# Ordering the engines' instructions by the library's detailed machine model

## The chip, the cores and the metric

The kernel runs on one core of a Trainium2 chip. The metric is the device time of one execution in microseconds (us), a median over runs.

## What is computed

Three blocks of a diffusion-style network run one after the other on 512 latent tokens and 256 context tokens of width 1024: a retention and state-space mixer with a gated feed-forward, an attention block with a feed-forward, and a second model's block with a recurrence over time, a short convolution and sixteen experts that each choose 64 tokens. Cut to the order of the work:

```python
h_lat = h_lat + m_lat[2] * retention_ssd_mixer(...)        # block 0, also for the context
h_lat = h_lat + m_lat[5] * swiglu(modulate(rms_norm(h_lat), ...), w_gate, w_up, w_down)
h_lat = h_lat + m_lat[2] * mla_mixer(...)                  # block 1
h_lat = h_lat + m_lat[5] * swiglu(...)
x = rms_norm(h_lat, final_norm_w)
x = x + g1 * (concat([rwkv_out(...), short_conv(...)]) @ w_out)   # second block
x = x + g2 * expert_choice_ffn(modulate(rmsnorm(x), ...), router_w, w_gate, w_up, w_down)
return rmsnorm(x)
```

## The kernel before

The kernel is traced once, as straight-line code, and nothing in it is a loop on the chip. Activations lie transposed, 128 features on the partitions and tokens along the free axis. Most products are made in three passes from a high and a low part of both operands: `gemm` issues the passes (L430, L432, L435), and `split_to` makes the parts, the high one on ScalarE (`act`, L382) and the low one on VectorE (`tt`, L385; on GpSimd where the caller says so). All helpers record their instructions under their own line, so L382, L385 and L388 (`stt`) stand for many places.

Memory is handed out by the kernel's own code while it is traced. `_Arena` gives out stretches of SBUF and `_Banks` gives out the eight banks of PSUM, both in the order of the trace. A stretch that was freed and given out again makes its next writer wait for its last reader. All loads and stores are issued by SyncE (`load`, L400; the experts' weights, L2594), so they form one queue in order.

Work that may overlap is traced interleaved: `braid` and `weave` step several generators at fixed rates, and `step` puts pieces of side work (`ada_rows`, which reads the transposed modulation weights `wadt` and sums products on VectorE, L668) between the blocks of the feed-forward `ffn`. `ffn` works in groups of hidden blocks (`FFG`, six groups for each of two layers). Each group ends with the loads of its down weights (`wdown`).

Further lines that are named below:
- `ssd` in block 0: L1282 multiplies the masked scores of a chunk with the values, behind a decay chain over VectorE, ScalarE and GpSimd (`affine_select`, L1266 and L1268); L1301 is the state's product there. L952 to L954 are the value projection's products that run beside it.
- `rwkv_prep` in the second block: L1957 multiplies a masked product with the values; the mask is applied by GpSimd (L385 on POOL). L1897 and L1909 are its copies and chunk products.
- `tri_inverse`: VectorE inverts triangular blocks with transposes (L2014, L2029, L2037, L2038), and L2045 and L2055 combine the blocks on TensorE.
- `moe`: the experts' products (L2598) with weights that stream in.

The order in which each engine gets its instructions is not the traced order. When the trace is closed, the library plays the traced instructions on a model of the machine: an engine of the model takes, among the instructions whose operands are ready there, the one that was traced first. The order that comes out of this play is written into each engine's program and is fixed from then on. On the chip every engine goes through its program in order and waits on semaphores. Without a further argument the library uses its simple model.

Of the kernel before, what the change touches and what calls it, by code (L numbers as in the profile page):

```python
# [167 lines left out]
def _run(g):  # L168
    """a generator to its end -> what it returns"""
    try:  # L170
        while True:
            next(g)
    except StopIteration as e:
        return e.value


def _parts(t):
    """two ranges of tokens"""
    return [(0, TL), (TL, TA)] if t == TA else [(0, TC), (TC, TL)]


class _Hook:
    """a generator step by step; what it returns"""
# [19 lines left out]
class _Arena:  # L203
    """SBUF, float32 left of a movable bound and float32r right of it, each side a stack of tiles.
    Long-lived buffers lie at the outer ends, transient ones rotate near the bound.
    Zones set memory aside for work that other work is to overlap."""
# [37 lines left out]
    def move(self, mid, *cuts):  # L244
        """float32 up to mid floats, float32r behind; new tiles end at the cuts"""
# [18 lines left out]
    def reserve(self, z, n, dt=F32, below=SIZE):  # L264
        """set n floats aside for zone z"""
# [48 lines left out]
    def forget(self, n):  # L314
        """the order of the last releases alone counts from here on"""
# [45 lines left out]
class _K:  # L361
# [50 lines left out]
    def prefetch(self, key, src):  # L412
        """split weights ahead of their use"""
        self.pre[key] = self.wsplit(src, top=True)
# [10 lines left out]
    def gemm(self, w, nk, acts, outs):  # L425
        """outs: list of (psum AP, token slice); w: function (hi|lo, k) -> lhsT; acts: list of (hi, lo) per k"""
# [22 lines left out]
    def rstd_cols(self, cols, n, scale, eps, op=OP.add):  # L449
        """1 / sqrt(cols * scale <op> eps), with a Newton step behind the square root's table"""  # L450
# [11 lines left out]
    def rms_bcast(self, acc, t, nfeat):  # L462
        """acc [128, t]: sums of squares per partition; -> bank with 1/rms on every partition"""
# [9 lines left out]
    def col_bcast(self, r, n):  # L473
        """[128, n] -> bank with the n * 128 values along each partition"""
# [6 lines left out]
    def sumsq(self, blocks, t, w=None, bufs=None, pool=None):  # L481
        """sum over blocks of squares, [128, t]; with w a second one, of the blocks times columns of w"""
# [21 lines left out]
    def modulate(self, xs, t, pb, segs, us=None, dve=()):  # L504
        """xs: list of f32 [128, t]; segs: list of (slice, scale fn(k), shift fn(k)); us: two APs for the normed values or
        None; -> list of (hi, lo) Bufs"""
# [17 lines left out]
    def norm_parts(self, xs, t, nfeat, segs, pool=0, low=((), ())):  # L524
        """normed and modulated blocks, range of tokens by range -> list of (hi, lo) Bufs"""
# [12 lines left out]
    def modulate_part(self, outs, xs, t0, t1, r, segs, low=()):  # L538
        """low: the blocks whose low part is left to GpSimd"""
# [22 lines left out]
    # log1p(e) for 0 <= e <= 1, elementwise on small tiles  # L562
# [31 lines left out]
    def ada(self, parts, w=2):  # L594
        """parameters of layer 0 -> Buf [128, 48, 2]: block-major vectors, (latent, context); params 1 and 4 are 1 + scale"""
# [30 lines left out]
    def ada_first(self, h):  # L626
        """half h of the blocks of layer 0's first shift and scale"""
# [15 lines left out]
        # block 8 j + 4 h + n at column (n, j, v)  # L643
# [8 lines left out]
    def ada_rows(self):  # L652
        """the same for layers 1 and 2 (context: shift and scale 0 alone), as VectorE's sums of products along the rows of
        the transposed weights"""
# [37 lines left out]
    # ---------------------------------------------------------------- layer 0  # L692
# [49 lines left out]
    def gated(self, x, p, P, gate, n, t0, t1, two):  # L742
        """x += gate * p over a range of tokens"""
# [5 lines left out]
    def out_proj(self, w, y, T, x, P, gate, k0=0, name=None, hook=None):  # L749
        """x += gate * (rows k0... of w)^T y; with a hook range of tokens by range, and the hook behind each"""  # L750
# [28 lines left out]
    def step(self, g, n, z=1):  # L779
        """n steps of work in a zone"""  # L780
# [8 lines left out]
    def ffn(self, l, P, T, x, a, side, rate, start=0, hook=None):  # L789
        """x += gate * swiglu(a); a: normed blocks as (hi, lo) Bufs; the last sums range of tokens by range, with a hook  # L790
        behind each"""
# [5 lines left out]
        def outs(bg, bu, bc, t0, t1):  # L797
            """gate's and up's PSUM over a range of tokens"""
# [27 lines left out]
        for g, nb in enumerate(FFG):  # L826
            j0 = 0
            last = g == len(FFG) - 1
            if g == 0:
                # the first two blocks range by range: the second range's norm is under way  # L830
# [55 lines left out]
    def mixer0(self, ab, P):  # L886
# [7 lines left out]
        # dt, [16, tokens]  # L894
# [1846 lines left out]
```

## Time and profile before

| | |
|---|---|
| median of 3 runs | 3152.22 us (3151.61 to 3154.9) |
| span of the profiled execution | 3154.1 us |
| TensorE busy | 2976.9 us (94%) |
| VectorE busy | 1702.1 us (54%) |
| ScalarE busy | 989.3 us (31%) |
| GpSimd busy | 312.5 us (10%) |
| mean granted TensorE clock | 0.947 |
| read from HBM | 441.35 MB |

The profile is of one execution. [...] A wait row names the waiting engine and line, and behind the arrow what came last of the things it waited for. A timeline row stands for one or more instructions of one line and one form in a row; the bracket gives the idle time of the engine ahead of it. "SPq" is the issue of a DMA by SyncE.

### The profile page before, as it was taken

The numbers are of one execution on the slowest core, as the hardware profiler recorded it, in microseconds if no ns is written. First come the engines' busy times: TensorE is split into PE (matmuls) and PEld (weight loads), VectorE is DVE, ScalarE is ACT, GpSimd is POOL, SyncE is SP. The second block draws the span as 40 slices with busy tenths as digits, with TensorE's granted clock in tenths as the row PEclk, the third lists the DMA queues.
The fourth block names the chain that finished last, engine by engine and source line by source line (L and its number), as shares of the span: only waits on it lengthen the run. The fifth ranks groups of instructions, "written<-read, shape, count | busy, mean of one in ns | idle before, by whom it ended". The sixth has DMA issues, their size and how long they took to land.

```text
span 3154.1 us, 43364 instructions
## 1 busy us (share of the span) xinstructions
PE 2976.9 (94%) x17688; PEld 2113.3 (67%) x17688; DVE 1702.1 (54%) x2713; ACT 989.3 (31%) x1625; POOL 312.5 (10%) x287
## 2 busy tenths in 40 slices
PE   7999999999999989999999999988899998999997
PEld 4776558888888877554788777775675565344443
DVE  5865557675764355565755762388636734112113
ACT  5421445412121165333544422244323313000001
POOL 0124310000000010111000000002201311000000
PEclk9999999999999999999999999888888877999999
DMA  6334451474563031001322222131113124999998
GB/s 216 106 103 124 137 175 58 152 257 157 165 226 134 11 125 40 22 22 45 108 95 74 95 79 75 34 108 64 55 38 106 41 85 173 377 409 409 409 409 303
DMA packets 170584, 458.97 MB, mean 146 GB/s; under 512 B 20320, under 2 KB 52704, under 8 KB 170000
## 3 DMA queue, kind: packets, MB, share of 16 engines
q1 hardware_dynamic: 170384, 456.19, 41.0%
q8 instruction: 139, 2.28, 0.3%
q14 instruction: 61, 0.50, 0.0%
HBM read 441.35 MB, written 14.78 MB: 145 GB/s over the span
## 4 chain that ended last, share of the span: by engine, by line
PE 71%; DVE 9%; DMA 5%; issue 3%; ACT 3%; POOL 2%; SPq 0%; DVEq 0%; POOLq 0%; ACTq 0%
PE ps L430 13%; PE ps L432 12%; PE ps L435 12%; PE ps L2598 9%; DVE mem L385 4%; ACT mem L382 3%; PE ps L1614 3%; PE ps L1773 2%; PE ps L2581 2%; DMA mem<-in_wadt_dram 2%; DVE mem L388 1%; POOL mem L385 1%; PE ps L1771 1%; PE ps L606 1%; PE ps L2258 1%
## 5 line engine op out<-in xcount | busy, mean ns | idle before, releaser
L382 ACT ACTIVATE mem<-mem 128x1024 fp32r<-128x1024 f32 (+16 forms) x802 | 543.2, 707 | 850.0 <-PE ps L435 225.3
L385 DVE TENSOR_TENSOR mem<-mem,mem 128x1024 fp32r<-128x1024 f32 (+13 forms) x595 | 515.5, 882 | 394.3 <-ACT mem L382 197.4
L382 ACT ACTIVATE mem<-ps 128x512 f32<-128x512 f32 (+8 forms) x627 | 321.0, 525 | 1130.8 <-PE ps L435 318.4
L430 PE MATMUL ps<-mem,mem 128*128 128x512 f32 (+3 forms) x1991 | 601.4, 359 | 16.1 <-ACT mem L382 13.1
L432 PE MATMUL ps<-mem,mem 128*128 128x512 f32 (+2 forms) x1906 | 569.4, 354 | 1.0 <-DVE mem L385 0.9
L435 PE MATMUL ps<-mem,mem 128*128 128x512 f32 (+2 forms) x1977 | 417.8, 352 | 0.0
L430 PEld LDWEIGHTS ps<-mem,mem 128*128 128x128 f32 (+2 forms) x1991 | 339.9, 189 | 88.0 <-ACT mem L382 19.6
L432 PEld LDWEIGHTS ps<-mem,mem 128*128 128x128 f32 (+1 forms) x1906 | 327.9, 189 | 59.9 <-issue 5.9
L435 PEld LDWEIGHTS ps<-mem,mem 128*128 128x128 f32 (+1 forms) x1977 | 323.7, 189 | 56.2 <-issue 4.1
L2598 PE MATMUL ps<-mem,mem 128*64 128x512 f32 x1344 | 309.2, 598 | 1.0 <-ACT mem L382 0.5
L385 POOL TENSOR_TENSOR mem<-mem 128x256 f32<-128x256 f32 (+4 forms) x84 | 106.1, 1269 | 1810.6 <-ACT mem L382 1411.2
L432 PE MATMUL ps<-mem 128*128 128x512 f32 (+1 forms) x814 | 275.1, 368 | 1.4 <-POOL mem L385 1.0
L430 PE MATMUL ps<-mem 128*128 128x512 f32 (+1 forms) x729 | 258.2, 378 | 10.1 <-ACT mem L382 7.8
L385 DVE TENSOR_TENSOR mem<-mem,ps 128x512 f32<-128x512 f32 (+5 forms) x234 | 128.9, 582 | 236.0 <-PE ps L2598 103.5
L385 DVE TENSOR_TENSOR mem<-mem 128x256 f32<-128x256 f32 (+19 forms) x347 | 186.6, 546 | 85.3 <-ACT mem L382 36.2
L2598 PEld LDWEIGHTS ps<-mem,mem 128*64 128x64 f32 x1344 | 107.1, 137 | 177.9 <-issue 165.7
L385 POOL TENSOR_TENSOR mem<-mem,mem 128x512 f32<-128x512 f32 (+6 forms) x108 | 145.3, 1357 | 515.4 <-ACT mem L382 402.1
L432 PEld LDWEIGHTS ps<-mem 128*128 128x128 f32 x814 | 154.9, 197 | 30.9 <-issue 4.4
L435 PE MATMUL ps<-mem 128*128 128x512 f32 (+3 forms) x743 | 170.7, 359 | 0.0
L430 PEld LDWEIGHTS ps<-mem 128*128 128x128 f32 x729 | 141.5, 199 | 43.5 <-ACT mem L382 12.7
L385 DVE TENSOR_TENSOR mem<-ps,mem 128x512 f32<-128x512 f32 (+6 forms) x176 | 114.2, 664 | 98.3 <-PE ps L1107 37.0
L388 DVE SCALAR_TENSOR_TENSOR mem<-ps,mem 128x256 f32<-128x256 f32 (+1 forms) x232 | 114.8, 534 | 96.8 <-PE ps L435 96.2
(303 smaller groups left out, 3091.0 us busy)
## 6 DMA issues: line engine op xcount, KB each, us to landing
mem<-in_eg_dram SPq DMA_DIRECT2D x128, 512.0 KB, 10.2
mem<-in_eu_dram SPq DMA_DIRECT2D x128, 512.0 KB, 10.2
mem<-in_ed_dram SPq DMA_DIRECT2D x128, 512.0 KB, 10.2
mem<-in_wadt_dram SPq DMA_DIRECT2D x96, 512.0 KB, 4.3
mem<-in_wup_dram SPq DMA_DIRECT2D x44, 512.0 KB, 3.5
mem<-in_wgate_dram SPq DMA_DIRECT2D x44, 512.0 KB, 3.5
mem<-in_wdown_dram SPq DMA_DIRECT2D x40, 512.0 KB, 3.5
mem<-in_w2in_dram SPq DMA_DIRECT2D x35, 512.0 KB, 3.6
```

The costliest lines, as they stand in the source:

```text
L382: return self.nc.scalar.activation(out, in_, func, **kw)
L385: return (eng or self.nc.vector).tensor_tensor(out, a, b, op=op)
L388: return self.nc.vector.scalar_tensor_tensor(out, a, s, b, op0=op0, op1=op1)
L430: mm(o, w(0, k), acts[k][0][:, ts], start=(k == 0), stop=False)
L432: mm(o, w(0, k), acts[k][1][:, ts], start=False, stop=False)
L435: mm(o, w(1, k), acts[k][0][:, ts], start=False, stop=(k == nk - 1))
L606: nc.tensor.matmul(b.a[32 * q:32 * q + 32, :], cs.a[:, k, :], raw.a[:, j * 512:(j + 1) * 512], start=(k == 0), stop=(k == 7))
L1614: mm(po.a[64 * i:64 * i + 64, :], v.a[:, kb, 64 * h:64 * h + 64], pt.a[:, i, :], start=(kb == 0), stop=(kb == 5))
L1771: self.nc.tensor.transpose(out, src, i)
L1773: self.nc.tensor.matmul(out, src, i, start=True, stop=True)
L2581: mm(b.a[:, :256], ht.a[:, c, fs], o, start=(c == 0), stop=(c == 3))
L2598: mm(bk.a[64 * i:64 * i + 64, 512 * n:512 * n + 512], lhs(k, i), w[i][:, 512 * n:512 * n + 512], start=(k == 0), stop=(k == 7))
```

## The change

One argument is added where the trace is opened. The rest of the diff takes comments and docstrings away.

```diff
 def _build(nc, I, out, dump=None):
-    with tile.TileContext(nc) as tc:
+    with tile.TileContext(nc, schedule_with_timeline_sim=True) as tc:
         with (tc.tile_pool(name="ps", bufs=1, space=PSUM) as pp,
               tc.tile_pool(name="dr", bufs=1, space=bass.MemoryType.DRAM) as dp):
...
-        cfg = [(0, 1, 32, 0, 32), (3, 2, 0, 32, 0)]   # (rows quadrant, columns quadrant, U cols, D0 cols, D1 cols)
+        cfg = [(0, 1, 32, 0, 32), (3, 2, 0, 32, 0)]
```

With it the library plays the same traced instructions on its detailed model of the machine. No instruction is added or removed by the kernel's code, and every tile keeps its place in SBUF and PSUM, since these were handed out during the trace. What can differ is the order of the instructions in each engine's program, SyncE's queue of loads included, and the semaphore waits that follow from it.

## Rows read from the trace of the kernel before

**Rows 1.** Page: the span, and busy time, share and instructions of each engine.

```profile
span 3154.1 us, 43364 instructions
...
PE 2976.9 (94%) x17688; PEld 2113.3 (67%) x17688; DVE 1702.1 (54%) x2713; ACT 989.3 (31%) x1625; POOL 312.5 (10%) x287
```

**Rows 2.** Windows: length, busy us of PE, PEld, DVE, ACT, POOL; clock, DMA, GB/s.

```profile
500.00:1000.00 500.00, 490.79 (x2789) 425.87 (x2788) 333.61 (x573) 128.29 (x184) 2.03 (x2) 0.99 0.51 171
2000.00:2500.00 500.00, 444.30 (x3819) 329.04 (x3818) 335.75 (x580) 172.26 (x317) 88.31 (x80) 0.85 0.20 65
2500.00:2660.00 160.00, 144.72 (x1436) 98.95 (x1436) 70.00 (x159) 43.90 (x93) 24.23 (x28) 0.76 0.33 113
2660.00:3154.00 494.00, 466.63 (x2132) 214.87 (x2130) 90.38 (x163) 51.02 (x96) 1.27 (x1) 0.98 0.96 376
...
2100.00:2200.00 100.00, 90.18 (x489) 66.54 (x487) 85.64 (x139) 42.33 (x64) 12.93 (x12) 0.95 0.30 99
2400.00:2500.00 100.00, 84.57 (x678) 48.34 (x678) 91.77 (x142) 35.38 (x68) 36.48 (x33) 0.87 0.29 94
```

**Rows 3.** Waits of TensorE, whole span: total us, times, longest us.

```profile
PE ps L1957 <- POOL mem L385: 22.6, 11, 5.8
...
PE ps L1282 <- issue: 10.7, 4, 3.5
...
PE ps L2045 <- DVE mem L2037: 4.5, 1, 4.5
...
PE ps L1301 <- DVE mem L385: 3.7, 3, 2.3
...
PE ps L2045 <- DVE mem L2029: 2.0, 1, 2.0
```

**Rows 4.** The same view in 700:1000 and in 2205:2500.

```profile
PE ps L430 <- ACT mem L382: 9.1, 3, 5.7
...
PE ps L1957 <- POOL mem L385: 16.9, 10, 5.0
```

**Rows 5.** Timeline at 1838:1854: start, us, engine, line, tiles, count, idle before.

```profile
1839.80 8.60 DVE L2029 STREAM_TRANSPOSE mem<-mem 32x1024 f32<-32x1024 f32 x4
...
1843.47 1.06 ACT L382 ACTIVATE mem<-mem 128x1024 fp32r<-128x1024 f32 x1 [5.63 <-DMA mem<-in_wdown_dram]
...
1851.56 1.91 PE L2045 MATMUL ps<-mem 32*32 32x32 f32 x32 [4.54 <-DVE mem L2037]
...
1853.40 0.80 PE L430 MATMUL ps<-mem,mem 128*128 128x512 f32 x1
```

**Rows 6.** Timeline at 711:726, where a down weight comes late.

```profile
714.34 0.33 SPq L400 DMA_DIRECT2D mem<-in_wadt_dram  x1
715.48 7.78 SPq L400 DMA_DIRECT2D mem<-in_wdown_dram  x2
...
724.76 1.65 PE L430 MATMUL ps<-mem,mem 128*128 128x512 f32 x4 [5.68 <-ACT mem L382]
```

**Rows 7.** Timeline at 2227:2231.5, VectorE beside GpSimd.

```profile
2227.51 0.74 DVE L388 SCALAR_TENSOR_TENSOR mem<-mem,mem 128x504 f32<-128x504 f32 x1
2227.65 3.62 POOL L385 TENSOR_TENSOR mem<-mem,mem 128x512 f32<-128x512 f32 x2 [10.14 <-ACT mem L382]
...
2228.16 0.32 DVE L385 TENSOR_TENSOR mem<-mem,mem 128x156 f32<-128x156 f32 x1
2228.39 1.75 DVE L388 SCALAR_TENSOR_TENSOR mem<-mem,mem 128x504 f32<-128x504 f32 x1
...
2230.06 1.38 DVE L385 TENSOR_TENSOR mem<-mem,mem 128x156 f32<-128x156 f32 x1
```

**Rows 8.** Windows at half clock behind those waits: two of seven, and the sum.

```profile
722.30:729.10 6.80, 4.34 (x13) 3.66 (x14) 3.71 (x5) 1.90 (x2) 0.00 (x0) 0.50 0.21 77
1848.70:1862.30 13.60, 10.74 (x108) 9.05 (x109) 7.06 (x7) 3.46 (x6) 0.00 (x0) 0.50 0.24 78
...
sum 47.60, PE 38.59 PEld 32.43 DVE 23.34 ACT 10.99 POOL 9.73; mean PE 5.51 PEld 4.63 DVE 3.33 ACT 1.57 POOL 1.39
```

## The prediction, made before the changed kernel ran

> **What bounds the kernel now.** I read the page first, then windows by stage, then TensorE's waits, and last the timeline around the longest of them. The page says that TensorE is the bound: busy 2976.9 of 3154.1 us, with VectorE at 54% and the others below [rows 1]. So 177.2 us of the span are idle on TensorE, and nothing that leaves TensorE as it is can move the time by much. The windows split this [rows 2]. In the feed-forward of block 0 (500 to 1000) TensorE is busy 490.8 of 500 us at full clock: little is to be had. From 2660 to the end the experts' weights stream in at 376 GB/s with the DMA engines 96% busy, and TensorE is busy 466.6 of 494: two limits at once, and the order of the same loads changes neither. In the second block (2000 to 2500) TensorE is idle for 55.7 us, its clock is 0.85, and in two of these five stretches VectorE is busy 85.6 and 91.8 of 100 us. From 2500 to 2660 the clock is 0.76. What an order can give or take lies there, and in single waits of block 0.
>
> **The change, part by part.** No instruction goes or comes, so there is no work to price. What is moved is each engine's order, and with it each wait of an engine that stands at an instruction whose operands are late while a later one of its program could run. So the terms are waits of that kind. I followed the operands of the instructions that stand behind each wait of TensorE of 0.5 us or more: where a later TensorE instruction had all its producers done, the wait is one of order; where none had, it is one of dependence, and no order of TensorE's mends it.
>
> Waits of order, with their sums:
> - L1282 and L1301 in the state-space part, 10.7 and 3.7 us [rows 3]. TensorE stands before a product whose decay chain is not done, with the value projection's products (L952 to L954) behind it.
> - L1957 in the second block, 16.9 of its 22.6 us [rows 3, 4]. It waits for a mask applied by GpSimd, with blocks of the input projection (L430, L432) behind it. The remaining 5.7 us are one wait with almost nothing ready.
> - L2045, 4.5 and 2.0 us [rows 3]. This one shows best what a wrong estimate does [rows 5]: VectorE's four transposes at L2029 take 8.60 us, 2.15 each. TensorE's program has L2045 next, so it stands 4.54 us, and then runs L430, whose high weights were written by ScalarE by 1844.53, before the wait began.
> - L430 at three ends of groups in the feed-forward, 9.1 us [rows 4]. Here the down weight is issued at 715.48, behind the queue's other loads, and TensorE starts on it at 724.76 [rows 6].
>
> The sum is 10.7 + 3.7 + 16.9 + 4.5 + 2.0 + 9.1 = 46.9 us.
>
> The clock is a second term. Behind seven of these waits TensorE runs at half clock for 47.6 us together, and is busy in 38.6 of them [rows 8]. At full clock the same work takes half, so 19.3 us hang on these waits too. Short stretches at half clock behind other waits, and those in stages of small products, are left alone.
>
> If all of it came back, the gain would be 46.9 + 19.3 = 66.2 us: 3154.1 - 66.2 = 3087.9. The median of the runs lies 1.9 us under the profiled span, which itself lies inside the runs' range, so nothing else stands around the span and I take these 1.9 off: 3086.0.
>
> How much of it comes back no row tells, because no row shows the detailed model at work. The ends are nothing and all. Outside the second block the waits sum to 46.9 - 16.9 = 30.0 us, and I take half, 15.0: the nearest row is L2045's, where the mispriced producer is plain, but the L430 ends are partly a chain of load, split and product that stays. For L1957 I take a quarter, 4.2: VectorE is the busiest engine next to these waits [rows 2], so TensorE, once it has filled such a wait, meets VectorE's results later on; VectorE is what is late next. That is 19.2 of 46.9, 41%, and the same share of the clock term is 7.9. Together 27.1 us: 3154.1 - 27.1 - 1.9 = 3125.1. I forecast 3125 us.
>
> What the new order moves apart from this: SyncE's queue of loads is also made anew, and every load that is moved ahead of another makes that one wait for its buffer too. VectorE's, ScalarE's and GpSimd's programs are reordered as well; their idle time is large, so they cost nothing until they feed TensorE late. These costs can only be bounded, and they are the rivals. About 6 us, 0.2%, is what a measurement of this kernel can tell from no change.
>
> **The rivals.** First, the load queue turns against the feed-forward, and the kernel gets slower. All loads pass one queue in order. The feed-forward has six ends of groups in each of two layers, twelve, and today three of them show a wait [rows 4]. If the new queue puts side loads (`wadt`) or early gate and up weights ahead of a down weight whose buffer is already free, each end costs what the worst one costs today: 5.7 us of standing [rows 4, 6] and half of the 4.3 us of TensorE's work at half clock behind it [rows 8], 7.9 together. With n such ends the change is 7.9 n, less the 9.1 + 2.2 of today, less the 27.1 - 4.6 - 0.9 = 21.6 gained elsewhere (4.6 is half of 9.1, 0.9 is 41% of 2.2). It breaks even at n = 4; with eight it is 63.2 - 11.3 - 21.6 = +30.3, so 3182.5 us. For it: the side loads wait for VectorE's products, and their number is unchanged. Against it: the stretch is 98% busy now [rows 2], and a model that knows when loads land has less reason to put them wrongly.
>
> Second, VectorE and GpSimd get in each other's way more often. A VectorE operation of 128x156 takes 0.32 us alone and 1.38 beside a GpSimd operation, and one of 128x504 takes 0.74 and 1.75 [rows 7]: about 1.0 us a time. From 2000 to 2660 GpSimd is busy 112.5 us [rows 2], at 1.8 us an operation [rows 7] about 62 operations. If three quarters of them, 46, newly delay a VectorE operation that TensorE waits for, the change is +46 - 27.1 = +18.9 and the time 3171 us. It decides from 27 such operations on. Against it: many of them collide already. [...]
>
> Third, nothing to be measured. The traced order comes first among ready instructions in either play, buffers and banks are fixed, and 130.3 of the 177.2 idle us are not waits of order by my reading. If less than 6 us come back net, or if the two models give nearly the same order, the time is 3152. Against it: the waits of order above are plain mistakes of the present order.
>
> **How the numbers follow.** Forecast (3125) 0.50, load queue (3182) 0.24, port (3171) 0.13, nothing (3152) 0.13. Faster is 0.50, same 0.13, slower 0.37. The range reaches from everything back, 3086, to 3186, just over the load queue's price; a larger gain, where VectorE's and ScalarE's own orders shorten chains, and a price at more than eight ends are left out. The forecast's own range is 3086 to 3146.
>
> **What would show it.** If the steps are right, the waits at L1282, L1957, L2045 and L430's ends shrink from 46.9 us to some 28, TensorE's idle time falls from 177 towards 158, the mean granted clock from 2000 to 2500 rises above 0.85, and the stretch from 2660 to the end keeps its 494 us. The forecast is wrong if the idle time stays and only changes lines, if L430 waits for ScalarE behind a late load at more than four ends, or if VectorE's two-input operations beside GpSimd grow longer in sum. It is also wrong if TensorE's busy time changes by more than the clock term: then the order has moved the clock's level for other reasons than the waits that I counted.

## The result, and the profile after

The changed kernel takes 3240.58 us (median of 4 runs, 3237.05 to 3245.33) against 3153.56 us for the kernel before beside it (4 runs, 3151.61 to 3155.82). The ratio is 1.0281, 95% interval 1.0265 to 1.0296: 87 us slower. The forecast was 3125 us with a range of 3086 to 3186, so the sign was wrong and the time lies outside the range.

The page of the changed kernel, as in [rows 1]:

```profile
span 3234.9 us, 43351 instructions
...
PE 3001.2 (93%) x17688; PEld 2131.4 (66%) x17688; DVE 1699.4 (53%) x2713; ACT 988.0 (31%) x1622; POOL 302.5 (9%) x287
```

The profiled spans differ by 80.8 us. TensorE's idle time grew from 177.2 to 233.7 us, by 56.5, and its busy time by 24.3 with the same 17688 records. So two things have to be explained, and the prediction had a term for the first alone.

TensorE's waits after, the view of [rows 3] (total us, times, longest):

```profile
PE ps L430 <- ACT mem L382: 41.4, 16, 6.1
PE ps L1909 <- ACT mem L382: 16.2, 2, 15.5
...
PE ps L952 <- ACT mem L382: 9.6, 1, 9.6
...
PE ps L2215 <- DVE mem L388: 6.4, 1, 6.4
...
PE ps L1282 <- DVE mem L385: 6.0, 2, 3.5
...
PE ps L1957 <- POOL mem L385: 4.3, 2, 3.1
```

The waits that the prediction named did shrink, as [rows 3] shows beside these: L1957 from 22.6 to 4.3, L1282 from 10.7 to 6.0 (it now stands for VectorE), and L2045 from 6.5 to 0.3. Others took their place. All waits of TensorE of 0.5 us and more make 152.9 us before and 207.3 after. Sorted by their operands as in the prediction, which no single view shows, they hold 56.6 us before and 41.0 after in which later work stood ready, but 96 and 166 us in which nothing did.

To see where the time went, both traces are cut at the same pieces of work: the last L952, the last L1301, the first L1187, L1474 (the start of the attention), the last L1614 (its end), the last L435, the last L2117 (the end of the recurrence). Windows of the kernel before, cut so (length, then busy us of PE, PEld, DVE, ACT, POOL, TensorE's granted clock as a share of full speed, DMA, GB/s):

```profile
0.00:168.00 168.00, 145.19 (x743) 106.23 (x744) 115.72 (x163) 84.09 (x125) 21.00 (x38) 0.98 0.46 155
168.00:278.20 110.20, 97.72 (x590) 82.39 (x590) 81.08 (x80) 24.70 (x32) 44.49 (x27) 0.97 0.40 110
278.20:478.60 200.40, 195.14 (x913) 114.95 (x912) 98.33 (x111) 77.37 (x98) 49.56 (x27) 0.96 0.48 156
478.60:1192.30 713.70, 695.07 (x3896) 597.98 (x3894) 436.05 (x759) 211.51 (x323) 12.03 (x11) 0.99 0.41 140
1192.30:1511.50 319.20, 305.55 (x1211) 175.80 (x1210) 192.02 (x228) 134.00 (x238) 49.28 (x44) 0.98 0.12 36
1511.50:2404.30 892.80, 846.60 (x6120) 677.08 (x6120) 528.87 (x915) 327.30 (x556) 74.15 (x78) 0.92 0.22 72
2404.30:2599.40 195.10, 179.67 (x1878) 111.80 (x1877) 121.90 (x193) 54.76 (x107) 46.46 (x47) 0.81 0.26 84
2599.40:3154.10 554.70, 511.95 (x2348) 247.12 (x2348) 128.15 (x266) 75.54 (x150) 15.53 (x15) 0.96 0.91 355
```

The same of the changed kernel, cut at the same pieces:

```profile
0.00:175.40 175.40, 141.09 (x743) 105.64 (x744) 110.65 (x159) 77.78 (x120) 17.24 (x37) 0.94 0.43 143
175.40:313.10 137.70, 114.89 (x668) 94.99 (x667) 85.41 (x87) 29.50 (x40) 49.37 (x31) 0.94 0.34 96
313.10:509.40 196.30, 177.79 (x819) 97.99 (x817) 98.19 (x107) 76.17 (x95) 46.65 (x26) 0.95 0.50 160
509.40:1237.90 728.50, 703.66 (x3910) 606.28 (x3910) 438.11 (x760) 209.09 (x321) 12.19 (x11) 0.97 0.41 137
1237.90:1582.10 344.20, 323.85 (x1212) 177.09 (x1211) 189.73 (x228) 134.87 (x238) 47.10 (x44) 0.97 0.11 34
1582.10:2438.40 856.30, 828.61 (x5755) 665.57 (x5754) 525.38 (x897) 328.43 (x552) 66.45 (x72) 0.92 0.23 75
2438.40:2681.30 242.90, 199.18 (x2282) 132.17 (x2282) 126.00 (x223) 58.15 (x119) 47.93 (x53) 0.80 0.23 74
2681.30:3234.90 553.60, 512.09 (x2309) 251.70 (x2308) 125.96 (x254) 73.97 (x143) 15.57 (x15) 0.96 0.91 353
```

Line by line the lengths change by +7.4, +27.5, -4.1, +14.8, +25.0, -36.5, +47.8 and -1.1, which is the 80.8. Block 0 and its feed-forward lose 45.6, the attention 25.0, and the experts' end keeps its time. The sixth and the seventh row must be read together: 6120 and 1878 matmul records before, 5755 and 2282 after, so the new order runs some 370 records behind the last L435 that ran ahead of it before. Part of the -36.5 and of the +47.8 is this work. The two rows together lose 11.3 us, of which 9.8 are idle time: TensorE's idle time falls by 18.5 us in the first (46.2 to 27.7) and rises by 28.3 in the second (15.4 to 43.7). In the attention the same work (x1211 and x1212 records) is busy 18.3 us longer, at a granted clock of 0.97 against 0.98, and 6.7 us more are idle.

### The profile page after: what moved, and what is told of

Its sections match the earlier page's. It is cut to its first block, busy times and chain, and to the rows that moved or that the text cites. A ratio compares the mean times of both kernels' runs of the same rounds, so it can differ in the third digit from the quotient of the medians.

```text
span 3234.9 us, 43351 instructions
## 1 busy us (share of the span) xinstructions
PE 3001.2 (93%) x17688; PEld 2131.4 (66%) x17688; DVE 1699.4 (53%) x2713; ACT 988.0 (31%) x1622; POOL 302.5 (9%) x287
## 4 chain that ended last, share of the span: by engine, by line
PE 70%; DVE 10%; DMA 6%; ACT 3%; issue 2%; SPq 0%; DVEq 0%; ACTq 0%
PE ps L430 13%; PE ps L432 12%; PE ps L435 12%; PE ps L2598 9%; DVE mem L385 5%; PE ps L1614 3%; ACT mem L382 3%; PE ps L2581 2%; DMA mem<-in_wadt_dram 2%; PE ps L1773 2%; PE ps L2258 1%; DMA mem<-in_eu_dram 1%; DVE mem L388 1%; DMA mem<-in_ed_dram 1%; PE ps L1607 1%
## 5 line engine op out<-in xcount | busy, mean ns | idle before, releaser
L382 ACT ACTIVATE mem<-mem 128x1024 fp32r<-128x1024 f32 (+12 forms) x802 | 543.3, 707 | 898.4 <-PE ps L435 205.5
L382 ACT ACTIVATE mem<-ps 128x512 f32<-128x512 f32 (+9 forms) x627 | 321.2, 526 | 1147.3 <-PE ps L435 326.0
L430 PE MATMUL ps<-mem,mem 128*128 128x512 f32 (+3 forms) x1991 | 600.6, 358 | 26.4 <-ACT mem L382 20.4
L432 PE MATMUL ps<-mem,mem 128*128 128x512 f32 (+3 forms) x1906 | 574.9, 355 | 1.0 <-DVE mem L385 1.0
L435 PE MATMUL ps<-mem,mem 128*128 128x512 f32 (+2 forms) x1977 | 419.9, 352 | 0.0
L430 PEld LDWEIGHTS ps<-mem,mem 128*128 128x128 f32 (+2 forms) x1991 | 342.1, 190 | 98.5 <-ACT mem L382 26.3
L432 PEld LDWEIGHTS ps<-mem,mem 128*128 128x128 f32 (+2 forms) x1906 | 329.9, 190 | 56.8 <-issue 4.1
L435 PEld LDWEIGHTS ps<-mem,mem 128*128 128x128 f32 (+1 forms) x1977 | 324.1, 190 | 58.7 <-issue 5.3
L2598 PE MATMUL ps<-mem,mem 128*64 128x512 f32 x1344 | 319.6, 596 | 1.5 <-ACT mem L382 0.6
L430 PE MATMUL ps<-mem 128*128 128x512 f32 (+1 forms) x729 | 256.7, 378 | 21.1 <-ACT mem L382 21.0
L2598 PEld LDWEIGHTS ps<-mem,mem 128*64 128x64 f32 x1344 | 114.1, 136 | 180.6 <-issue 164.6
L385 DVE TENSOR_TENSOR mem<-mem 128x256 f32<-128x256 f32 (+21 forms) x347 | 183.2, 537 | 80.4 <-ACT mem L382 41.0
L430 PEld LDWEIGHTS ps<-mem 128*128 128x128 f32 x729 | 142.9, 201 | 54.2 <-ACT mem L382 27.6
L435 PE MATMUL ps<-mem 128*128 128x512 f32 (+3 forms) x743 | 168.8, 357 | 0.0
L388 DVE SCALAR_TENSOR_TENSOR mem<-ps,mem,mem 128x512 f32<-128x512 f32 (+2 forms) x130 | 79.6, 655 | 154.8 <-ACT mem L382 99.8
```

What stands on the lines that cost most here:

```text
L382: return self.nc.scalar.activation(out, in_, func, **kw)
L385: return (eng or self.nc.vector).tensor_tensor(out, a, b, op=op)
L388: return self.nc.vector.scalar_tensor_tensor(out, a, s, b, op0=op0, op1=op1)
L430: mm(o, w(0, k), acts[k][0][:, ts], start=(k == 0), stop=False)
L432: mm(o, w(0, k), acts[k][1][:, ts], start=False, stop=False)
L435: mm(o, w(1, k), acts[k][0][:, ts], start=False, stop=(k == nk - 1))
```

## The experiments

All kernels below trace the same instructions and do the same work. The order that each model gives is read back, and ordering edges of a kind without semaphores (`NoSync`) hold engines in a given order. That the edges themselves cost nothing is seen in x6 and x17 below: both hold every engine by such edges, in the order of before but for one edit, and take the time of before (1.0004 and 0.9998). This part is common ("..." stands for lines left out):

```diff
-def _build(nc, I, out, dump=None):
-    with tile.TileContext(nc) as tc:
+def _build(nc, I, out, dump=None, detailed=False, pins=()):
+    with tile.TileContext(nc, schedule_with_timeline_sim=detailed) as tc:
...
+            traced = list(bb.instructions)
+            for chain in pins:
+                for p, q in zip(chain, chain[1:]):
+                    tc.add_manual_dep(traced[q], traced[p].name, mybir.DependencyInfo(
+                        mybir.DependencyClass.NoSync, mybir.DependencyReason.DATA), reason="pin")
```

Names such as I-9520 are those of single instructions. Ratios are to the kernel before, with 95% intervals; where one is turned into us, it is multiplied by 3153.6.

### One wait mended: the time comes back next door

In the changed kernel's recurrence TensorE's longest new wait is the 15.46 us at L1909. The timeline shows why: VectorE works through the triangular inverse's chain of small products, the group norm's small operation (L453) stands behind them, ScalarE's queue waits for that, and TensorE for ScalarE.

```profile
2529.80 22.53 DVE L385 TENSOR_TENSOR mem<-mem 128x60 f32<-128x60 f32 x46
...
2552.45 0.22 ACT L382 ACTIVATE mem<-mem 128x16 f32<-128x16 f32 x1 [14.05 <-DVE mem L453]
...
2555.87 3.68 PE L1909 MATMUL ps<-mem 64*64 64x128 f32 x32 [15.46 <-ACT mem L382]
```

```diff
+    order, eng, name = detailed
...
+    for what, behind in (("I-16711", "I-16272"), ("I-16713", "I-16331"), ("I-16714", "I-16332"),
+                         ("I-16715", "I-16333"), ("I-16716", "I-16334")):
+        order.remove(name.index(what))
+        order.insert(order.index(name.index(behind)) + 1, name.index(what))
+    return [[k for k in order if eng[k] == e] for e in sorted(set(eng))]
```

> The changed kernel's order on every engine, with one edit: five small VectorE operations of the group norm (the L453 group whose result ScalarE waits 14.05 us for at 2538 to 2552) stand some 30 places earlier in VectorE's queue, among the triangular inverse's chain of small products in place of behind it. Theory of queues (a wait that the new order added comes from the place of one operation in an in-order queue, and is gained back where that place is mended): TensorE's wait of 15.46 us at L1909 goes, 3240.6 - 15.5 = 3225, and up to 6 us less if the slow clock behind it goes too (3219 to 3227). Theory of spent cover (independent products were used up early, and the time comes back as idle time at the next chain): the wait goes, the later ones grow, 3236 to 3241.

Measured: 1.0317 (1.0294 to 1.0340), so 3249 us by the median or 3254 by the ratio, and no gain. The waits in 2500 to 2740 of this run begin so:

```profile
PE ps L2215 <- DVE mem L388: 24.7, 1, 24.7
...
PE ps L1909 <- ACT mem L382: 2.7, 2, 1.9
```

The longest wait at L1909 fell from 15.5 to 1.9, and the one at L2215, the group norm's next matmul, rose from 6.4 to 24.7: together 21.8 before the edit and 26.6 with it. What TensorE lacked here was work. The lines view of the kernel before, over its inverse (2460 to 2515), against the changed kernel's (2528 to 2572), shows which:

```profile
L1773 PE MATMUL ps<-mem,mem 64*64 64x64 f32 x64 | 14.0, 316 | 0.0
L2258 PE MATMUL ps<-mem,mem 128*128 128x512 f32 x16 | 11.3, 862 | 0.0
L1771 PE MATMUL ps<-mem,mem 64*64 64x64 f32 x32 | 9.5, 295 | 0.0
L2258 PE MATMUL ps<-mem 128*128 128x512 f32 x12 | 6.2, 627 | 0.0
```

```profile
L1909 PE MATMUL ps<-mem 64*64 64x128 f32 x96 | 7.7, 321 | 15.5 <-ACT mem L382 15.5
...
L1771 PE MATMUL ps<-mem,mem 64*64 64x64 f32 x4 | 1.0, 261 | 0.0
L1773 PE MATMUL ps<-mem,mem 64*64 64x64 f32 x6 | 1.0, 242 | 0.0
```

Before, the output projection (L2258, 17.5 us) and 96 small products of L1771 and L1773 ran while VectorE inverted. In the changed order no L2258 is left for that time, since 64 of its 96 had run from 2467 on, and 10 of the others.

### One queue held: worse than both

Followed back by operands (again shown by no single view), the added waits of TensorE ended mostly at operations that stood in ScalarE's queue (3.3 us before, 33.3 after) and at late loads (19.3 and 42.0). If so, the queue concerned should give them back when it is held in the order of before:

```diff
+    order, eng, _ = simple
+    return [[k for k in order if eng[k] == "SP"]]
...
+    simple, detailed = _program(arrays)[1], _program(arrays, detailed=True)[1]
+    nc, _ = _program(arrays, detailed=True, pins=_pins(simple, detailed))
```

This is x3; x4 has "Activation", ScalarE, in place of "SP".

> The detailed model orders the engines, but SyncE's queue, which issues all loads, is held in the kernel before's order. Followed back by operands, TensorE's waits of 0.5 us and more came from loads for 19.3 us before and 42.0 us after. Theory of queues: these 22.7 us go, and with them 4 to 9 us of slow clock behind the waits: 3209 to 3218. Theory of spent cover: the order of the loads is not the cause, 3234 to 3246.

Measured: 1.0376 (1.0358 to 1.0394).

> The detailed model orders the engines, but ScalarE's queue is held in the kernel before's order. Followed back by operands, 33.3 us of TensorE's waits of 0.5 us and more came from operations that stood ready in ScalarE's queue behind others, against 3.3 us before. Theory of queues: these 30 us go, and up to 12 us of slow clock with them: 3198 to 3211. Theory of spent cover: the waits come back at the bare chains, 3230 to 3245.

Measured: 1.0594 (1.0576 to 1.0613).

Both theories missed: the one kernel is 30 us slower than the changed one, the other 100. In the first the stretch up to the last L435 rose from 293.2 to 341.0 us behind L1719, in the second the attention's from 343 to 384. But these runs do not hold the other engines: the model plays them anew around the held queue, and the traces show other orders. TensorE's row of matmuls departs from the changed kernel's at the 55th, and of 17688 records 13844 stand at their old place in x3 and 11325 in x4. So the runs time two further orders, and whether the late loads or ScalarE's queue make the added waits stays open. From here on every engine is held: whole orders are exchanged, or single places are moved.

### Whole stretches exchanged

```diff
...
+    parts = ((order, "I-9520"), (detailed[0], "I-15880"), (order, None))
+    line, seen = [], set()
+    for o, last in parts:
+        o = o[:o.index(name.index(last)) + 1] if last else o
+        line += [k for k in o if k not in seen]
+        seen.update(o)
+    return [[k for k in line if eng[k] == e] for e in sorted(set(eng))]
```

I-9520 is the last L1614 and I-15880 the last L435. The other runs of this kind differ in `parts` alone: x8 is `((order, "I-15880"), (detailed[0], None))`, and x7, x13 and x14 are `((detailed[0], ...), (order, None))` up to I-7928 (L1474), I-1357 (the last L952) and I-1201 (the last L1301).

> The kernel before's order on every engine up to the last L1614, then the changed kernel's order up to the last L435, then the kernel before's for all that is left. In the two traces this middle stretch took 892.8 us before (1511.5 to 2404.3) and 856.3 us after (1582.1 to 2438.4), and the stretch behind it, to the end, 749.8 and 796.5. If each stretch's time follows from its own order: 3153.6 - 36.5 = 3117. If the middle stretch is shorter because it uses up products that the recurrence behind it needs as cover: the stretch behind it grows by as much, 3150 to 3165, though its order is again that of before.

Measured: 0.9979 (0.9964 to 0.9994), 6.6 us faster. The stretch and the one behind it, up to the last L2117:

```profile
1509.26:2364.63 855.37, 827.65 (x5756) 664.94 (x5757) 525.55 (x897) 328.42 (x552) 64.89 (x72) 0.93 0.23 75
2364.63:2579.85 215.22, 192.49 (x2243) 124.18 (x2243) 131.06 (x211) 56.51 (x112) 48.48 (x53) 0.83 0.24 78
```

The stretch is 37.4 us shorter than before and the next one 20.1 longer, 12.8 of it busy time for the 365 records that were handed on and 7.3 idle. Together they gain 17.3 us in this profile and 6.6 by the medians. So neither number of the expectation came, and its 36.5 was a wrong price to begin with: it took moved work for gained time.

> The kernel before's order up to the last L435, then the changed kernel's order. That last stretch took 749.8 us before and 796.5 us after. If its own order makes the difference: 3153.6 + 46.7 = 3200. If it is slower because the stretch ahead of it had used up the products that cover its chains, it is so only in part here, where that stretch has the order of before: with the 20.2 us that the run with the detailed order in the stretch ahead alone gave back at this place taken off, 3180, or less.

Measured: 1.0105 (1.0083 to 1.0127), 33 us slower, between the two. The recurrence's row:

```profile
2397.61:2627.89 230.28, 185.94 (x1916) 119.05 (x1916) 118.62 (x205) 56.20 (x114) 43.06 (x47) 0.78 0.24 78
```

With the order of before ahead of it and nearly its work (1916 records against 1878) the stretch is 35.2 us longer than before, and TensorE is idle in it for 44.3 us, as in the changed kernel (43.7), against 15.4 before. So the loss in the recurrence is made by that stretch's own order; the stretch ahead hands on work to it, but little idle time (7.3 us in x2).

> The changed kernel's order up to L1474, the start of the attention, then the kernel before's order on every engine. In the two traces L1474 came at 1192.3 us before and 1237.9 us after. If the 45.6 us are lost by the order of that stretch and nothing later gives them back: 3199 (3195 to 3204). If a part of it was only work done earlier than before, which the later stretches then need not do: 3165 to 3185.

Measured: 1.0151 (1.0130 to 1.0173), 48 us: block 0 and its feed-forward lose theirs for good, whatever comes behind.

> The changed kernel's order up to the last L952, then the kernel before's order. TensorE's idle time up to there is 22.8 us before and 34.3 after (the two large ones among it are 6.1 us at L430 and 9.6 us at L952, both behind weights that were loaded and split late). If block 0's 46 us are lost stretch by stretch, each by its own order: 3153.6 + 11.5 = 3165, or 3161 by the landmark, which comes 7.4 us later. If this start sets back the chain that all of the mixer hangs on: 3180 to 3200.

Measured: 1.0079 (1.0058 to 1.0101), 25 us. The last L952 comes 7 us late here, and 13 us more are lost up to the last L1282 (87.6 us against 74.6, idle 18.8 against 8.7), although that part has the order of before. Its waits show the place (0 to 320; beside this row L1282 has 5.7 us "<- issue", where the kernel before has 0.8 and 10.7):

```profile
PE ps L1282 <- DVE mem L385: 12.3, 2, 11.4
```

> The changed kernel's order up to the last L1301, then the kernel before's order. Idle time up to there is 35.3 us before and 57.2 after, and the stretch behind it, up to the first L1187, has 5.3 before and 18.5 after. If each stretch loses by its own order: 3153.6 + 21.9 = 3175. If the end of the mixer runs bare because the matmuls that covered it had been used up before L1301 (the stretch ahead has 17 us more of busy time than in before): most of the 13.2 us are lost here too, though the order behind L1301 is that of before: 3184 to 3190.

Measured: 1.0070 (1.0049 to 1.0092), 22 us, no more than x13. The first theory had 3175 and is met in number (3176.2), but not in its reason: x13, with the first 175 us alone, lost as much. So the changed order between L952 and L1301 adds nothing that can be told: up to L1301 the loss comes from the first 175 us, which hand something late on to L1282. The other half of x7's 48 us, some 25, is made between L1301 and L1474 by the order there, nearly all of it in the feed-forward: 733.0 us in x7 against 710.4 in x14, with TensorE idle 26.8 against 14.1. So the expectation's other case for x14, a loss handed on behind L1301, did not come.

### Waits of order filled by hand: the prediction's mechanism alone

```diff
+    order, eng, name = simple
...
+    for to, what in FORWARD:
...
+        gone = set(what)
+        order = [k for k in order if k not in gone]
+        at = order.index(place["I-%d" % to])
+        order[at:at] = what
```

`FORWARD` lists, for each filled wait, the waiting instruction and the ready ones that go ahead of it.

> As the run with 25 places mended, but only the ten places of block 0's mixer (95 matmuls, 16.7 us of waits, the last four of them at L1301 and the five at L1282 before them). Theory of the prediction: 3153.6 - 16.7 = 3137, or 3145 if half is lost elsewhere. Theory of spent cover: the matmuls that go ahead at L1282 are the ones that stood beside the state chain of L1301, whose waits grow by as much: 3150 to 3156.

Measured: 1.0004 (0.9990 to 1.0018), nothing of 16.7 us. (The ten places are three ahead of L1282 with 2.3 us, four at L1282 with 10.7 and three at L1301 with 3.7; the expectation's split of them is miscounted, its sum is right.) The waits in 140 to 320, where the kernel before has 10.7 and 3.7 [rows 3]:

```profile
PE ps L1282 <- DVE mem L385: 7.5, 3, 6.2
...
PE ps L1301 <- DVE mem L385: 4.3, 4, 1.6
PE ps L1282 <- issue: 3.9, 2, 3.0
```

The filled waits (L1282 <- issue) fell from 10.7 to 3.9, and the same line then waits 7.5 us for VectorE where it had waited 0.8: 11.5 in sum before, 11.4 now. The last L952 comes 8.5 us earlier, and the stretch from there to the last L1282 is 10.0 us longer. By these waits the chain over VectorE sets the pace here, and TensorE only waits at one place or another; no run here shortened that chain.

> The prediction's own mechanism by itself: the kernel before's order on every engine, and on TensorE 247 matmuls that stood ready behind a waiting one go ahead of it, at 25 places; the waits of order that this fills add up to 43.1 us in the trace of before (among them 9.7 us at L1282, 5.5 of them behind the first, 2.3 us at L1301, 4.5 us at L2045, 7.9 us at L1957). Theory of the prediction (a filled wait of order is gained, with some slow clock behind it): 3153.6 - 43.1 = 3110, or 3132 if half of it is lost elsewhere. Theory of spent cover (the matmuls moved ahead are missing as cover later): 3143 to 3154.

Measured: 0.9944 (0.9924 to 0.9964), 18 us faster, between the two. As block 0's ten places give nothing, the other fifteen give it, with 26.4 us of waits filled. In the profile most of it lies between L1719 and the last L435, before and in this run:

```profile
2078.50:2404.30 325.80, 296.70 (x2534) 230.03 (x2533) 206.29 (x349) 106.75 (x182) 43.26 (x39) 0.86 0.20 67
```

```profile
2074.50:2379.50 305.00, 285.50 (x2533) 221.79 (x2533) 206.75 (x349) 106.43 (x182) 40.85 (x39) 0.90 0.21 72
```

With the same work the stretch is 20.8 us shorter: 9.6 of idle time, where waits of 9.9 us at L1957 and L2045 were filled, and 11.2 of busy time, as the granted clock rises from 0.86 to 0.90. Here the fill came back whole, and the clock with it. Four of the fifteen places lie in block 0's feed-forward, and there the fills gave little: its row of 713.7 us takes 711.9 in this run.

### Two matmuls next to each other

What is left is the attention, 25.0 us with 18.3 of them busy. L1614 multiplies the exponentials with the values of two heads, one into the upper and one into the lower 64 partitions of a bank, each with 64 columns of TensorE. In the program of the kernel before, 31 of the 48 pairs stand next to each other, in the changed one 5 (the expectation's 8 or 9 is a miscount). The timeline of the kernel before (each matmul has two records):

```profile
1407.73 1.35 PE L1614 MATMUL ps<-mem,mem 128*64 128x512 f32 x4
1409.02 0.50 PE L1607 MATMUL ps<-mem,mem 97*128 97x512 f32 x1
1409.35 0.40 PE L1608 MATMUL ps<-mem,mem 96*128 96x512 f32 x1
1409.60 0.40 PE L1609 MATMUL ps<-mem,mem 96*128 96x512 f32 x1
1409.83 0.40 PE L1607 MATMUL ps<-mem,mem 97*128 97x512 f32 x1
```

And of the changed kernel:

```profile
1399.65 1.07 PE L1614 MATMUL ps<-mem,mem 128*64 128x512 f32 x2
...
1401.55 1.07 PE L1614 MATMUL ps<-mem,mem 128*64 128x512 f32 x2
```

Two together take 1.35 us here, a lone one 1.07. The expectations and the text below count to the start of the next matmul, and then a lone one takes 1.00.

```diff
...
+    pe = [k for k in order if eng[k] == "PE"]
+    for a, b in PAIRS:
+        a, b = place["I-%d" % a], place["I-%d" % b]
+        pe.remove(a)
+        pe.insert(pe.index(b), a)
...
```

> The changed kernel's order on every engine, with one edit on TensorE: the two 64-column matmuls of L1614 that belong to one block of keys stand next to each other, 48 pairs, where the changed kernel has 8 or 9 pairs so and the kernel before 31. In the traces a lone one took 1.00 us (34 groups of before, all within 1.00 to 1.04) and two next to each other 1.62 us on average (1.01 at the least), and all of L1614 84.4 us before and 91.9 after. Theory of pairs (two next to each other run side by side): some 40 pairs more, 0.4 us each at before's average, 0.99 at best: 3241 - 16 = 3225 (3200 to 3231). Theory that the attention's 25 us are the slow clock and the waits, and the neighbours don't matter: 3236 to 3246.

Measured: 1.0131 (1.0111 to 1.0150) in place of the changed kernel's 1.0281: 47 us back, more than the theory's best (43 pairs were apart and not 40, which would make 43). The attention's stretch falls from 343 to 300.5 us (counted from L1474's end, 1 us less than in the table), at a granted clock of 0.94 against 0.97, and all of L1614 falls from 91.9 to 52.6 us, 1.10 a pair. The lines view of L1614's main form (168 of 192 records), before, after and in this run:

```profile
L1614 PE MATMUL ps<-mem,mem 128*64 128x512 f32 x168 | 77.6, 627 | 0.9 <-ACT mem L382 0.8
```

```profile
L1614 PE MATMUL ps<-mem,mem 128*64 128x512 f32 x168 | 88.6, 626 | 1.5 <-ACT mem L382 1.5
```

```profile
L1614 PE MATMUL ps<-mem,mem 128*64 128x512 f32 x168 | 48.3, 627 | 0.0
```

The mean of one record stays at 627 ns; how many of them run side by side changes. This shows what the pairs are worth, but it does not price the 25.0 us: all 48 pairs stand together here, 17 more than in the kernel before. From before to after L1614 grew by 7.5 us to the next start (84.4 to 91.9; by 12.9 in the lines view with its smaller form), and L1624, the attention's other product of 64 columns, by 4.2 in that view (15.5 to 19.7). The kernel before has much of the same to gain. In x10 the first of a pair stands in front of the second, in x11 both stand three matmuls behind the second's old place:

> The kernel before's order, with the first matmul of each of the 48 pairs of L1614 directly in front of the second one. 17 pairs more than before stand together. Theory of pairs: 17 times 0.4 to 0.99 us, 3153.6 - 7 to 17 = 3137 to 3147. No effect of neighbours: 3150 to 3157.

Measured: 0.9959 (0.9944 to 0.9973), 13 us faster, as the theory said. All 48 pairs stand next to each other, and yet one takes 1.49 us on average: in 40 of them the second matmul starts 0.1 us or more behind the first, each time 0.05 us after the end of a ScalarE operation, so it waits for the exponentials that it reads. In the kernel before this holds for 29 of the 31.

> The kernel before's order, with each of the 48 pairs of L1614 together and three matmuls later, so that the exponentials that both read are there when the pair starts. Theory of pairs: nearly all pairs take the 1.01 us of the best ones of before, 48 x 1.01 = 48.5 in place of 84.4 us: 3153.6 - 36 = 3118 (3115 to 3135, if a part turns into waits for the exponentials). No effect of neighbours: 3150 to 3157.

Measured: 0.9944 (0.9929 to 0.9959), 18 us of the 36 expected. The pairs do take 1.07 us each (51.2 us for all 48), but TensorE's idle time in the attention grows to 23.8 us from 13.7, so part of the gain turned into waits. Only one second matmul is still seen to start late: standing together is not enough, the second's operand has to be there as well.

> The pairs of L1614 together and three matmuls later, and the 15 places outside block 0's mixer where matmuls go ahead of a waiting one (26.4 us of waits, of which the run with 25 places gained about 20). If the two add up: 3153.6 - 36 - 20 = 3098 (3095 to 3117). If the gain at the waits is lost again: 3115 to 3135.

Measured: 0.9875 (0.9854 to 0.9896), 39 us faster: what x11 and x5 gained adds up (18 and 18), though not to the 56 expected.

> As the run with pairs and 15 mended places, but the pairs of L1614 stand one matmul later in place of three. With three, the pairs took 1.04 us each and the attention's stretch 299.7 us, of which TensorE is idle 23.6 us against 13.7 before; with none, 1.49 us and 306.3 us with 15.7 idle. If the idle time comes from the places behind the pairs (the scores wait for a bank that the exponentials hold): 3108 to 3114. If not, between the two: 3114 to 3120.

Measured: 0.9870 (0.9853 to 0.9888). The idle time in the attention falls to 17.5 us, but L1614 takes 59.7 us where it took 50.4 in x12, and the stretch 299.6 us as with three places (299.7): no difference that can be told.

### A chain brought forward on one engine

Block 0's start holds a chain of small VectorE operations on 16 partitions (`dt` and its decay sums), which ends with a store through SyncE (L1228), at 119.16 us before and 134.75 after. The edit sets its links one other operation apart.

```diff
...
+    stretch = [place["I-" + n] for n in STRETCH.split()]
+    at = iter(stretch)
+    order = [next(at) if k in set(stretch) else k for k in order]
...
```

> The changed kernel's order on every engine, with one edit on VectorE: in block 0's start the links of dt's chain (the operations on 16 partitions between L567 and L1213) stand closer together, with one other operation between two of them where there were two to four, and those others come later. By the durations in the trace the chain then ends at 119.8 us in place of 134.7 (119.1 in the kernel before). If this chain sets the pace of block 0's mixer and its lateness is what the run with the changed order up to L952 lost (some 25 us): 3241 - 15 = 3226, down to 3216. If it is the loads and the splits at L430 and L952 instead, or the later stretches: 3236 to 3246.

Measured: 1.0280 (1.0255 to 1.0306), nothing.

> The kernel before's order with the same edit on VectorE: the links of dt's chain one other operation apart, so that the chain ends at 112.3 us in place of 119.1 by the durations in the trace. If the chain sets the pace of block 0's mixer (there filled waits of TensorE gained nothing): 3153.6 - 7 = 3147. If TensorE's work sets it: 3152 to 3156.

Measured: 0.9998 (0.9986 to 1.0010), nothing. x16's timelines of VectorE and SyncE say that the edit did not reach its aim:

```profile
120.51 1.00 DVE L388 SCALAR_TENSOR_TENSOR mem<-mem 16x768 f32<-16x768 f32 x1
```

```profile
135.24 0.33 SPq L400 DMA_DIRECT2D mem<-in_w0in_dram  x1
135.62 0.42 SPq L1228 DMA_DIRECT2D scratch<-mem  x1
```

VectorE ended the chain at 121.5 us, 13 us earlier than in the changed kernel, but SyncE's queue has a weight load in front of the store, which waited for its buffer until 135.24. In x17 the first store went out at 116.47 in place of 119.16, but the last one of the three (L1229) at 131.91 in place of 130.23. So these two runs leave open whether the chain, if it were early on all its queues, would give block 0's first 25 us back.

> All edits that paid, in the kernel before's order: 15 mended places, the pairs of L1614 together and one matmul later, and dt's chain closer together. The run without the chain's edit took 0.987 of the kernel before, 3113 of 3153.6. If the chain sets block 0's pace: 3106. If not: 3111 to 3116.

Measured: 0.9863 (0.9847 to 0.9879), not to be told from x15. Both are about 42 us faster than the kernel before and some 130 faster than the changed one. x18's page has TensorE busy 2941.2 of 3108.9 us, 36 us less than before with the same records.

## Why the prediction was wrong

**The bound.** TensorE's idle time was the right thing to look at, and it did decide: 56.5 of the profiled 80.8 us. The experts' end kept its time as said (494.6 and 494.9 us behind the first L2581).

**The step that failed.** The step is the one that sorts the waits. The prediction split TensorE's waits into those of order and those of dependence, and let the change act on the first alone; the 130.3 us of the second kind were taken as fixed. They are not: a new order makes new ones. The waits with ready work behind them fell by 15.6 us, about what the forecast had (19.2), while those with nothing ready rose by 70. At one place the runs show how: 28 matmuls of L2258 ran beside the inverse before, none after (2529 us); the chain that they had covered runs bare, and mending its longest wait only moved it (x1). That a fill must cost its cover is not the rule, since 18 us stayed in x5; and the recurrence's idle time comes from its own order (44.3 us in x8, with the order of before ahead of it), hardly from the stretch ahead (22.7 in x2, against 15.4 before). For the other added waits the cause is not shown. The prediction also put the new programs of the other engines and the late loads at nothing in its sum, and waits at operations that stood ready in ScalarE's queue rose from 3.3 to 33.3 us, those at late loads from 19.3 to 42.0; x3 and x4 did not decide whether these made the loss.

**The share.** Half was taken for the waits outside the second block and a quarter for L1957. x6 and x5 measured it the other way round: nothing of block 0's 16.7 us, little in its feed-forward (1.8 us less in x5), and all of the 9.9 at L1957 and L2045. The reason given for the small share, that VectorE is busy there, did not settle it: VectorE is busy for 81.1 of the 110.2 us of block 0's mixer too (168 to 278). By x6's waits what counts is whether the chain itself sets the pace.

**The clock term.** It counted half the time at full clock. In the trace of before 128x512 matmuls start 0.43 us apart at a clock of 0.50 (1861.49 to 1861.92) and 0.23 apart at 1.00 (1862.55 to 1862.78), somewhat more than half. Where a fill stayed, this time did come back: 11.2 us of busy time in x5, with the clock at 0.90 for 0.86. For the whole changed kernel it has the wrong sign: the mean granted clock went from 0.947 to 0.939, and where the new waits stand it fell most: up to the last L952 to 0.94 from 0.98. From 2000 to 2500 it is 0.86, against the 0.85 of [rows 2].

**What had no term.** The order decides which 64-column matmuls meet. That is a part of the attention's 25.0 us: of its 18.3 us of busy time L1614 holds 7.5 to 12.9 and L1624 some 4, by the way of counting, while the 6.7 us of idle time are waits. The condition in the prediction's last sentence, busy time that changes by more than the clock, came true.

**The rivals.** A loss was given 0.37, by two mechanisms that did not make it where they were to. The load queue was to turn at the ends of the feed-forward's groups, where L430 waits for ScalarE behind a late load. From 478.6 to 1192.3 before, and from 509.4 to 1237.9 after, these waits are alike:

```profile
PE ps L430 <- ACT mem L382: 13.7, 7, 5.7
```

```profile
PE ps L430 <- ACT mem L382: 14.1, 6, 4.1
```

So it did not turn there, nor in the second layer's feed-forward: up to the last L1719 these waits are 0.7 us before and 2.5 after. Late loads did cost more elsewhere, as said above. VectorE and GpSimd did not get in each other's way more: VectorE's busy time is 1699.4 us against 1702.1. The rival's price was misread besides: GpSimd's first operation runs from 2227.65 to 2229.60, and the two rows called alone (0.74 and 0.32 us) lie beside it too [rows 7], so operations beside GpSimd are not always longer. "Nothing to be measured" fell with the result.

**The account.** Of the profiled 80.8 us, block 0 and its feed-forward make 45.6, the attention 25.0, the second block's two stretches together 11.3, and the end -1.1. The runs assign these: 22 to 25 of the 45.6 to the order of the first 175 us (x13, x14) and some 25 to the order behind L1301 (x7 less x14); of the attention's, a part to its pairs (x9 takes back more than all of it, by more pairs than the kernel before had); the second block's to the order of the recurrence, which loses 33 by itself (x8), against 7 to 17 gained by the order ahead of it (x2). These two leave 16 to 26 where 11.3 were profiled, so they do not add up exactly. Open is what in block 0's first 175 us sets the chain back, which waits make the 25 us behind L1301, and how much of the attention's 25.0 is the pairs alone.

## What to carry to other kernels

Before a wait is counted as a gain, ask which chain loses the work that fills it: here 26.4 us of fills gave 18 where TensorE had other work, and 16.7 gave nothing where, by its waits, a chain on another engine set the pace. A more detailed model does not make a better order by itself; take its order by stretches and time them. Look at which narrow matmuls stand next to each other, and whether both have their operands: in the kernel before that was worth as much as the filled waits (18 us each), and in the changed one 47 us.

## What the runs showed of the hardware

Two matmuls of 128x64 (f32 in the trace), one for the upper and one for the lower 64 partitions of a bank, ran side by side in these traces where they followed each other in TensorE's program and the second's operand was there in time: two took 1.01 us at the least, and a lone one 1.00 us (34 of them, 1.00 to 1.04). Two next to each other took 1.62 us on average before and 1.49 in x10, where 29 of 31 and 40 of 48 second ones started late, and 1.07 and 1.10 in x11 and x9. A full-width matmul right behind such a pair is followed by the next one 0.33 us later (1409.02 to 1409.35), where the next two steps are 0.25 and 0.23 (to 1409.83); what makes the 0.1 us is not shown.

In x16 SyncE's queue held a finished result back: a store whose data were there at 121.5 us was issued at 135.62, behind a load that waited for its buffer until 135.24.
